# Paired GLA levels, mLSTM work on GpSimd, another projection weight and shifted pools in one encoder layer

## Chip, cores and metric

The kernel runs on one core of a Trainium2 chip. The metric is the device time of one launch in microseconds (us). Before the change it is 1205.28 us, the median of three runs (1203.65 to 1209.78).

## What is computed

One layer of an encoder over T = 1024 positions of width D = 1024 in float32. Token mixing and channel mixing follow each other, each with an RMS norm ahead and behind and a residual add:

```python
hn   = rms_norm(x, norm_mix_pre)
proj = hn @ w_in            # a_qk 512, a_v 512, a_o 512, a_gates 16, b_q 256, b_k 256, b_v 512, b_r 512, b_lr 32
# group A: 4 mLSTM heads (dk 64, dv 128), forward and backward, summed
qk  = silu(dwconv3(a_qk)); h_fw, h_bw = mlstm_chunkwise(...)
y_a = sigmoid(a_o) * head_rms_norm(h_fw + h_bw)
# group B: 4 GLA heads (dk 64, dv 128), forward and backward, summed
la  = log_sigmoid(lr @ w2 + gb) / 16
y_b = silu(b_r) * head_rms_norm(o_fw + o_bw)
x   = x + rms_norm(concat(y_a, y_b) @ w_out, norm_mix_post)
hn  = rms_norm(x, norm_ffn_pre)
x   = x + rms_norm((gelu(dwconv3(hn @ w_gate)) * (hn @ w_up)) @ w_down, norm_ffn_post)   # D_FF 2816
```

Within a chunk, GLA weighs each pair of positions (t, s) by exp(b_t - b_s) for each of the 64 key dimensions, where b is the running sum of the log gates:

```python
diff  = b[:, :, None, :] - b[:, None, :, :]
decay = exp(where(causal, diff, -inf))
s = einsum('td,sd,tsd->ts', q, k, decay)
o = s @ v + (q * exp(b)) @ S
```

mLSTM's weight of a pair is one number per head, exp(b_t - b_s + i_s - m_t), with a running maximum m and a normaliser n.

## The kernel before, in words

**Precision.** Most matmuls are done on splits: an operand becomes a high part in f32r and a low part with the rest (`split`, L109 to 111, a copy on ScalarE and a subtraction on VectorE), and a product is three matmuls, high by high, high by low, low by high.

**Stages.** The trace's span falls into these stretches: until 45 us the norm of x, its transposes into `xh`, `xl` and the first projection block (`wh0`, `wl0` from pool `s1`, L259); until about 455 us the rest of the projection, interleaved with the whole of the mixing; until 586 us the out projection (L975); until 991 us gate and up projection of the MLP; until the end at 1209 the down projection (L1194).

**The interleaved stage.** Two generators are run by `_interleave` (L42): `proj()` and `mix()`. Each holds a sum; the one with the lower sum gets the next step, and its weight is added. `proj()` has the weight 0.25. `mix()` starts with 1.0 and yields new weights on its way: `W_AUX` 0.85 for the decays and gates (`gla_decay`, `gate_rows`), `W_GLA` 0.19 for `gla()`, `W_ML` 0.26 for `mlstm()`, `W_OUT` 0.5 for `out_weights()`. A weight of 0.26 thus gives the projection 1.04 steps for each yield of the mix. `proj()` has 192 steps. Nearly each has matmuls: a `t_block` (L174) makes 48 matmuls of 128x256 for a pair of 128-row blocks in steps of 12, an `f_block` (L163) 24 of 128x512 in steps of 6. What the mix leaves over is run behind it, up to the point where the gate columns are done (`done["gate"]`), which the out projection's `prep(0)` needs.

The order in which steps are emitted gives priority; an instruction that is ready can be moved ahead of others on its queue, DMAs above all. Loads and stores through SP's queue (SPq in the profile) wait until the buffer that they fill is free.

**gate_rows** (L299) computes mLSTM's gate rows, stores two of them to DRAM (`drr`, `dri`) and, in its last step, transposes `gi`, `gf` and `rm` for eight chunks into `cols` (`ptc`, L369).

**gla()** (L543) has chunks of 128 positions: levels of chunk 0, then the states of all chunks, then for each chunk the levels of the next and its own `finish`. `levels(c)` cuts the 128x128 triangle into blocks: for L = 64, 32, 16, 8, 4, 2, 1 it pairs neighbouring blocks of L positions. A level has POOL subtract a reference column from the log sums X (`Dt`, L612), ScalarE take two exponentials of halves with opposite signs into the PSUM tile `E` (L616, L617), VectorE multiply E with q and k (`Q`; `K` or one of the zeroed `kz` tiles, L630). Then it yields, and TensorE makes the 32- or 64-wide score blocks `sc` (L649). These are merged into `acc` and `Pt` by copies and `copy_predicated`. The diagonal (k against q, without weights) follows level 1 in the same step. A chunk has eight yields. `finish(c)` makes `o`, copies it to `ob`, takes its head norm (ScalarE squares, a `pow` on POOL, L540, into `hr`) and stores it.

**mlstm()** (L696): `states()` makes chunk states (`Um`, L742). Then `front(c + 1)` and `back(c)` alternate, a yield behind each. `front` loads k, q and v and broadcasts rows into `RB` (128x1024, two directions) and `RI`; it makes the scores `sr` (L768), adds the causal mask `cap` (part of tile `cin`) to RB on VectorE (L769), takes eight exponentials on ScalarE (L772), multiplies by `sr` on VectorE (L773), and multiplies `RI` by q on VectorE (L775). `back` makes `nd` from RB and v and from RI and the states (L784, L788), divides into `hs` (ScalarE L799, VectorE L800), takes the head norm and stores to `dya`.

**out_weights()** (L828) loads w_out in eight pieces (`oraw`, L835) and splits them into `woh`, `wol` (L106, L107). Its pool `op` is opened when mlstm's pools are closed and lies over them. `prep(0)` (L846) then loads y (`yv`) and the gates (`gv` from `dG`), multiplies (L855), transposes (L861) and splits into `yh`, `yl`.

**The MLP** uses one level of a Strassen-like scheme. `strassen` (L1073) makes seven products of four by three matmuls 128x512 (`product`, L1036) for each of 22 operand sets. The moving operands are B11 and B21 (pool `bp`), T1 to T4 and B22 (pool `tp`); the stationary ones, `ah` and `al`, lie in pool `fw`.

**Where tiles lie.** Pools are opened on the left or (`side="right"`) on the right of each partition's memory. The left has `cst` (ident, one, hg, hr, mhalf), then `s1`, `mid`, `rw`, `gp`, the mix's `lp` pools, `op`, `pre`, `ering`, `tp`, `fk` and the down projection's pools, one over another as they close. The right has `xt`, `wp`, `rst`, `stg` and later `bp`, `fw`, `nt`. A tile that is made longer in `cst` moves all later pools on the left.

## Time and profile before

| | before |
|---|---|
| median of three runs | 1205.28 us |
| lowest, highest | 1203.65, 1209.78 us |
| profiled execution, run time | 1211.2 us |
| its span | 1209.4 us |
| mean granted clock of TensorE | 0.987 |
| TensorE busy, matmuls | 1166.3 us (96%), 7896 |
| VectorE busy | 895.2 us (74%) |
| ScalarE busy | 601.0 us (50%) |
| POOL busy | 129.6 us (11%) |
| DMA | 175.77 MB, mean 145 GB/s |

The profile is one execution. Busy time counts instructions that run; a wait stands with the instruction that came behind it and with what released it. TensorE's matmuls are pipelined, so the time of one is longer than the distance from one start to the next, and a rate is read from starts. The granted clock is a share of TensorE's full speed.

### The profile page before, as it was taken

The numbers are of one execution on the slowest core, as the hardware profiler recorded it, in microseconds if no ns is written. First come the engines' busy times: TensorE is split into PE (matmuls) and PEld (weight loads), VectorE is DVE, ScalarE is ACT, GpSimd is POOL, SyncE is SP. The second block draws the span as 40 slices with busy tenths as digits, with TensorE's granted clock in tenths as the row PEclk, the third lists the DMA queues.
The fourth block names the chain that finished last, engine by engine and source line by source line (L and its number), as shares of the span: only waits on it lengthen the run. The fifth ranks groups of instructions, "written<-read, shape, count | busy, mean of one in ns | idle before, by whom it ended". The sixth has DMA issues, their size and how long they took to land.

```text
span 1209.4 us, 21264 instructions
## 1 busy us (share of the span) xinstructions
PE 1166.3 (96%) x7896; PEld 985.8 (82%) x7896; DVE 895.2 (74%) x1620; ACT 601.0 (50%) x1327; POOL 129.6 (11%) x167
## 2 busy tenths in 40 slices
PE   8998999989988899999999999999999999999997
PEld 8988777878887898887788888888888878888885
DVE  5576689677365547667998887888878877987666
ACT  5573786778556534446543233323333335444451
POOL 1201433554001100111000000000000000000001
PEclk8998999999999999999999999999999999999999
DMA  7453675553677467442144332333224228854345
GB/s 193 151 140 89 191 212 143 149 153 107 192 207 191 147 215 245 140 157 79 35 140 139 105 114 63 129 114 114 72 94 131 96 81 306 266 166 140 87 135 187
DMA packets 134651, 175.77 MB, mean 145 GB/s; under 512 B 24964, under 2 KB 89860, under 8 KB 134548
## 3 DMA queue, kind: packets, MB, share of 16 engines
q1 hardware_dynamic: 134116, 172.58, 46.4%
q0 software_dynamic: 432, 1.84, 0.4%
q8 instruction: 62, 1.02, 0.3%
q14 instruction: 41, 0.34, 0.1%
HBM read 126.78 MB, written 47.53 MB: 144 GB/s over the span
## 4 chain that ended last, share of the span: by engine, by line
PE 69%; DMA 3%; DVE 3%; ACT 1%; issue 1%; SPq 0%; POOL 0%; DVEq 0%; POOLq 0%; ACTq 0%
PE pr L1036 35%; PE pr L1194 17%; PE tacc L180 7%; PE oacc L975 6%; DMA RB<-drr 1%; PE nd L784 1%; PE pt L861 1%; DMA yv<-dya 1%; ACT RB L772 1%; PE Um L742 1%; PE sc L649 0%; DMA qq<-dmqq 0%; PE sr L768 0%; DMA v<-dva 0%; DMA ar<-dA 0%
## 5 line engine op out<-in xcount | busy, mean ns | idle before, releaser
L1036 PE MATMUL pr<-T,ah 128*128 128x512 f32 x704 | 222.1, 397 | 1.1 <-DVE G L1074 1.1
L1036 PE MATMUL pr<-B,ah 128*128 128x512 f32 x528 | 164.3, 392 | 0.0
L1036 PEld LDWEIGHTS pr<-T,ah 128*128 128x128 f32 x704 | 132.4, 188 | 33.4 <-DVE G L1074 1.5
L1036 PE MATMUL pr<-T,al 128*128 128x512 f32 x352 | 139.5, 396 | 0.0
L180 PE MATMUL tacc<-wh,xh 128*128 128x256 f32 x448 | 133.1, 297 | 0.0
L180 PE MATMUL tacc<-wl,xh 128*128 128x256 f32 x448 | 131.0, 292 | 0.0
L180 PE MATMUL tacc<-wh,xl 128*128 128x256 f32 x448 | 130.5, 291 | 0.0
L1194 PE MATMUL pr<-dwl,dah 128*128 128x512 f32 x308 | 120.0, 390 | 0.7 <-DVE dwl L111 0.7
L1194 PE MATMUL pr<-dwh,dal 128*128 128x512 f32 x308 | 120.0, 389 | 0.0
L1194 PE MATMUL pr<-dwh,dah 128*128 128x512 f32 x308 | 119.1, 389 | 0.6 <-ACT dah L110 0.6
L1036 PEld LDWEIGHTS pr<-B,ah 128*128 128x128 f32 x528 | 99.1, 188 | 22.3
L1036 PE MATMUL pr<-B,al 128*128 128x512 f32 x264 | 103.4, 392 | 0.0
L110 ACT CAST dah<-ar 128x512 fp32r<-128x512 f32 x77 | 47.7, 622 | 98.3 <-PE pr L1194 46.9
L180 PEld LDWEIGHTS tacc<-wh,xh 128*128 128x128 f32 x448 | 88.1, 197 | 3.0 <-issue 0.2
L180 PEld LDWEIGHTS tacc<-wl,xh 128*128 128x128 f32 x448 | 88.3, 197 | 0.8
L180 PEld LDWEIGHTS tacc<-wh,xl 128*128 128x128 f32 x448 | 88.2, 197 | 0.6
L110 ACT CAST ah<-fraw 128x512 fp32r<-128x512 f32 x64 | 39.7, 620 | 86.4 <-PE pr L1036 58.0
L111 DVE TENSOR_TENSOR dal<-ar,dah 128x512 fp32r<-128x512 f32 x77 | 52.7, 687 | 38.5 <-ACT dah L110 38.5
L1036 PEld LDWEIGHTS pr<-T,al 128*128 128x128 f32 x352 | 66.3, 188 | 16.1
L110 ACT CAST ah<-sa 128x512 fp32r<-128x512 f32 x44 | 27.3, 621 | 87.1 <-PE pr L1036 51.2
L1194 PEld LDWEIGHTS pr<-dwh,dah 128*128 128x128 f32 x308 | 57.8, 188 | 13.0 <-ACT dah L110 1.0
L1194 PEld LDWEIGHTS pr<-dwl,dah 128*128 128x128 f32 x308 | 57.8, 188 | 12.9 <-DVE dwl L111 1.1
(294 smaller groups left out, 2520.5 us busy)
## 6 DMA issues: line engine op xcount, KB each, us to landing
ar<-dA SPq DMA_DIRECT2D x77, 256.0 KB
wraw<-in_w_in_dram SPq DMA_DIRECT2D x48, 256.0 KB
fraw<-in_ffn_w_gate_dram SPq DMA_DIRECT2D x22, 512.0 KB
fraw<-in_ffn_w_up_dram SPq DMA_DIRECT2D x22, 512.0 KB
dA<-s SPq DMA_DIRECT2D x20, 512.0 KB
dA<-sx SPq DMA_DIRECT2D x10, 768.0 KB
Y<-in_ffn_w_down_dram SPq DMA_DIRECT2D x22, 256.0 KB
S<-dS SPq DMA_DIRECT2D x16, 258.0 KB
```

The lines of the kernel that those rows point to most:

```text
L110: nc.scalar.copy(out=hi, in_=src)
L111: nc.vector.tensor_tensor(out=lo, in0=src, in1=hi.bitcast(F32), op=ALU.subtract)
L180: nc.tensor.matmul(acc[:, i, :], v[:, k, ts], w[:, k, :], start=(k == 0 and n == 0), stop=(k == NK - 1 and n == 2))
L742: nc.tensor.matmul(U[:, j, 0:P + 1], KT[:, 2 * g + j, :], v[:, 2 * g + j, :], start=True, stop=True)
L772: nc.scalar.activation(RB[:, i, h, :], RB[:, i, h, :], AF.Exp, bias=cols[:, c, 0, 32 * i + h:32 * i + h + 1])
L784: nc.tensor.matmul(nds[h // 2][i][:, h % 2, 0:P + 1], Ps[i][:, h, :], v[:, h, :], start=(h % 2 == 0), stop=False)
L861: nc.tensor.transpose(pt[:, j, :], yv[:, (4 * g + j) * P:(4 * g + j + 1) * P], ident)
L975: nc.tensor.matmul(accs[hf], v[:, j, :], w[:, k, hf * 512:(hf + 1) * 512], start=(k == 0 and n == 0), stop=(k == NK - 1 and n == 2))
L1036: nc.tensor.matmul(acc, A[i][:, k, :], B[b][j][:, k, :], start=(k == 0 and n == 0), stop=(k == 3 and n == 2))
L1194: nc.tensor.matmul(accs[i], o[v][:, ts], o[w], start=(p == 0 and n == 0), stop=(p == NP - 1 and n == 2))
```

## The change

There are five edits.

1. `levels(c)`: a level's subtraction is written as two of half the size with opposite signs, so that one exponential over the whole tile serves both halves. The score products of two levels are issued together, one step behind the weighing of the second (`products(due[:2])`), and their merges behind both. The diagonal counts as a level of its own with a yield of its own, so a chunk has nine yields. Q has three buffers, ob one.
2. `gate_rows` has one more yield ahead of the transposes.
3. `W_ML` is 0.36, which gives 1.44 projection steps a yield.
4. In mLSTM's `front`, the mask add on RB and the product of RI and q are on POOL.
5. A tile of 152 float32 (608 bytes a partition) is added to `cst`, one of 168 (672 bytes) to `s1`. Nothing uses them.

```diff
--- before.py
+++ after.py
@@ -34,7 +34,7 @@
 TEMP = 16.0
 BIG = 1e30
 
-W_AUX, W_GLA, W_ML, W_OUT = 0.85, 0.19, 0.26, 0.5
+W_AUX, W_GLA, W_ML, W_OUT = 0.85, 0.19, 0.36, 0.5
 C_AQK, C_AV, C_AO, C_AG = 0, 512, 1024, 1536
 C_BQ, C_BK, C_BV, C_BR, C_LR = 1552, 1808, 2064, 2576, 3088
 
@@ -100,6 +100,7 @@
     hg = cst.tile([P, NK, 1], F32, name="hg")
     hr = cst.tile([P, NC, 2, H], F32, name="hr")
     mhalf = cst.tile([P, 8], F32, name="mhalf")
+    cst.tile([P, 152], F32, name="shift")
     nc.gpsimd.memset(mhalf, -0.5)
 
     def split_scaled(hi, lo, src, g):
@@ -205,6 +206,7 @@
     sml = rst.tile([P, NT, 112], F32, name="sml")
     s1c = ExitStack()
     s1 = s1c.enter_context(tc.tile_pool(name="s1", bufs=2))
+    s1.tile([P, 168], F32, name="shift0", bufs=1)
     wh0 = s1.tile([P, NK, NS], F32R, name="wh0", bufs=1)
     wl0 = s1.tile([P, NK, NS], F32R, name="wl0", bufs=1)
     gpre = s1.tile([P, D], F32, name="gpre", bufs=1)
@@ -363,6 +365,7 @@
             nc.sync.dma_start(ddec[i], dcr[rs, :])
             nc.sync.dma_start(dec[64 * i:64 * i + 64], ddec[i].rearrange("(o h) c -> o h c", o=1).broadcast_to([64, H, NC]))
         yield
+        yield
         for c in range(NC):
             pt = ps.tile([P, 3, 36], F32, name="ptc", tag="ps")
             for j, z in enumerate((gi, gf, rm)):
@@ -572,7 +575,7 @@
                     v = v_tile(lp, dvb, c)
                     nc.scalar.activation(gam[:, c, :], S[:, :, P], AF.Exp, scale=1.0 / TEMP)
                     E = edge_decay(S, hi, lo)
-                    kd = w2k("Q")
+                    kd = w2k("Q", 3)
                     nc.vector.tensor_tensor(out=kd, in0=E, in1=kk, op=ALU.mult)
                     yield
                     pt = ps.tile([P, H, P], F32, name="ptk", tag="ps")
@@ -604,64 +607,79 @@
                 X = S[:, :, 0:P]
                 Pt = w2k("Pt")
                 acc = lp.tile([P, H, 32], F32, name="acc")
-                mi = 0
-                for L in (64, 32, 16, 8, 4, 2, 1):
-                    nb = P // (2 * L)
+                half = lambda z, i, L: z.rearrange("p h (n i j) -> p (h n) i j", i=2, j=L)[:, :, i, :]
+
+                def weigh(L):
+                    if L == 0:
+                        return qq, kk
                     Dt = w2k("D")
-                    xv = X.rearrange("p h (n j) -> p h n j", j=2 * L)
-                    nc.gpsimd.tensor_tensor(out=Dt.rearrange("p h (n j) -> p h n j", j=2 * L), in0=xv,
-                                            in1=xv[:, :, :, L:L + 1].broadcast_to([P, H, nb, 2 * L]), op=ALU.subtract)
+                    xv, dv = (z.rearrange("p h (n i j) -> p h n i j", i=2, j=L) for z in (X, Dt))
+                    ref = xv[:, :, :, 1, 0:1].broadcast_to([P, H, P // (2 * L), L])
+                    nc.gpsimd.tensor_tensor(out=dv[:, :, :, 0, :], in0=ref, in1=xv[:, :, :, 0, :], op=ALU.subtract)
+                    nc.gpsimd.tensor_tensor(out=dv[:, :, :, 1, :], in0=xv[:, :, :, 1, :], in1=ref, op=ALU.subtract)
                     E = pe.tile([P, H, P], F32, name="E", tag="pe")
-                    half = lambda z, i: z.rearrange("p h (n i j) -> p (h n) i j", i=2, j=L)[:, :, i, :]
-                    nc.scalar.activation(half(E, 0), half(Dt, 0), AF.Exp, scale=-1.0 / TEMP)
-                    nc.scalar.activation(half(E, 1), half(Dt, 1), AF.Exp, scale=1.0 / TEMP)
-                    Q = w2k("Q")
+                    nc.scalar.activation(E, Dt, AF.Exp, scale=1.0 / TEMP)
+                    Q, K = w2k("Q", 3), None
                     if L == 64:
                         nc.vector.tensor_tensor(out=Q, in0=E, in1=z64, op=ALU.mult)
-                    elif L == 32:
-                        nc.vector.tensor_tensor(out=Q, in0=E, in1=qq, op=ALU.mult)
+                        return Q, K
+                    nc.vector.tensor_tensor(out=Q, in0=E, in1=qq, op=ALU.mult)
+                    if L == 32:
                         K = w2k("K", 1)
                         nc.vector.tensor_tensor(out=K, in0=E, in1=kk, op=ALU.mult)
                     else:
-                        nc.vector.tensor_tensor(out=Q, in0=E, in1=qq, op=ALU.mult)
                         K = kz[L]
                         for i in range(2):
                             rs = slice(64 * i, 64 * i + 64)
-                            nc.vector.tensor_tensor(out=half(K[rs], i), in0=half(E[rs], i), in1=half(kk[rs], i), op=ALU.mult)
-                    yield
-                    if L == 64:
-                        sc = ps.tile([P, H, 64], F32, name="sc", tag="ps")
-                        for h in range(H):
+                            nc.vector.tensor_tensor(out=half(K[rs], i, L), in0=half(E[rs], i, L), in1=half(kk[rs], i, L), op=ALU.mult)
+                    return Q, K
+
+                def pair_up(L, Q, K):
+                    sc = ps.tile([P, H, 64 if L == 64 else 32], F32, name="sc", tag="ps")
+                    for h in range(H):
+                        if L == 64:
                             nc.tensor.matmul(sc[0:64, h, :], Q[0:64, h, 0:64], Q[0:64, h, 64:128], start=True, stop=True)
                             nc.tensor.matmul(sc[64:128, h, :], Q[64:128, h, 64:128], Q[64:128, h, 0:64], start=True, stop=True)
+                            continue
+                        for b in range(4):
+                            bs = slice(32 * b, 32 * b + 32)
+                            if L == 32:
+                                ob = slice(32 * (b ^ 1), 32 * (b ^ 1) + 32)
+                                rs = lo if b % 2 == 0 else hi
+                                nc.tensor.matmul(sc[bs, h, :], K[rs, h, bs], Q[rs, h, ob], start=True, stop=True)
+                            elif L == 0:
+                                nc.tensor.matmul(sc[bs, h, :], kk[:, h, bs], qq[:, h, bs], start=True, stop=True)
+                            else:
+                                nc.tensor.matmul(sc[bs, h, :], K[:, h, bs], Q[:, h, bs], start=True, stop=True)
+                    return sc
+
+                def keep(L, sc):
+                    if L == 64:
                         nc.scalar.copy(out=Pt[0:64, :, 64:128], in_=sc[0:64])
                         nc.scalar.copy(out=Pt[64:128, :, 0:64], in_=sc[64:128])
+                    elif L == 32:
+                        for b in range(4):
+                            ob = slice(32 * (b ^ 1), 32 * (b ^ 1) + 32)
+                            nc.scalar.copy(out=Pt[32 * b:32 * b + 32, :, ob], in_=sc[32 * b:32 * b + 32])
+                    elif L == 16:
+                        nc.scalar.copy(out=acc, in_=sc)
                     else:
-                        sc = ps.tile([P, H, 32], F32, name="sc", tag="ps")
-                        for h in range(H):
-                            for b in range(4):
-                                bs = slice(32 * b, 32 * b + 32)
-                                if L == 32:
-                                    ob = slice(32 * (b ^ 1), 32 * (b ^ 1) + 32)
-                                    rs = lo if b % 2 == 0 else hi
-                                    nc.tensor.matmul(sc[bs, h, :], K[rs, h, bs], Q[rs, h, ob], start=True, stop=True)
-                                else:
-                                    nc.tensor.matmul(sc[bs, h, :], K[:, h, bs], Q[:, h, bs], start=True, stop=True)
-                        if L == 32:
-                            for b in range(4):
-                                ob = slice(32 * (b ^ 1), 32 * (b ^ 1) + 32)
-                                nc.scalar.copy(out=Pt[32 * b:32 * b + 32, :, ob], in_=sc[32 * b:32 * b + 32])
-                        elif L == 16:
-                            nc.scalar.copy(out=acc, in_=sc)
-                        else:
-                            nc.vector.copy_predicated(acc, bmask[:, mi:mi + 1, :].broadcast_to([P, H, 32]), sc)
-                            mi += 1
-                sc = ps.tile([P, H, 32], F32, name="sc", tag="ps")
-                for h in range(H):
-                    for b in range(4):
-                        bs = slice(32 * b, 32 * b + 32)
-                        nc.tensor.matmul(sc[bs, h, :], kk[:, h, bs], qq[:, h, bs], start=True, stop=True)
-                nc.vector.copy_predicated(acc, bmask[:, mi:mi + 1, :].broadcast_to([P, H, 32]), sc)
+                        mi = (8, 4, 2, 1, 0).index(L)
+                        nc.vector.copy_predicated(acc, bmask[:, mi:mi + 1, :].broadcast_to([P, H, 32]), sc)
+
+                def products(pair):
+                    scs = [(L, pair_up(L, *qk)) for L, qk in pair]
+                    for L, sc in scs:
+                        keep(L, sc)
+
+                due = []
+                for n, L in enumerate((64, 32, 16, 8, 4, 2, 1, 0)):
+                    due.append((L, weigh(L)))
+                    if n % 2 == 0 and n:
+                        products(due[:2])
+                        due = due[2:]
+                    yield
+                products(due)
                 for b in range(4):
                     bs = slice(32 * b, 32 * b + 32)
                     nc.scalar.copy(out=Pt[bs, :, bs], in_=acc[bs])
@@ -678,7 +696,7 @@
                 for h in range(H):
                     nc.tensor.matmul(o[:, h, :], Pt[:, h, :], v[:, h, 0:P], start=True, stop=False)
                     nc.tensor.matmul(o[:, h, :], qd[:, h, :], slots[:, c, h, :], start=False, stop=True)
-                ob = w2k("ob")
+                ob = w2k("ob", 1)
                 nc.scalar.copy(out=ob, in_=o)
                 head_norm(lp, ob, dyb[c], 1, c)
                 yield
@@ -766,13 +784,13 @@
                 sr = ps.tile([P, H, P], F32, name="sr", tag="ps")
                 for h in range(H):
                     nc.tensor.matmul(sr[:, h, :], kk[:, h, :], qq[0:64, h, :], start=True, stop=True)
-                nc.vector.tensor_tensor(out=RB, in0=RB, in1=cap.rearrange("p (i o t) -> p i o t", i=2, o=1).broadcast_to([P, 2, H, P]), op=ALU.add)
+                nc.gpsimd.tensor_tensor(out=RB, in0=RB, in1=cap.rearrange("p (i o t) -> p i o t", i=2, o=1).broadcast_to([P, 2, H, P]), op=ALU.add)
                 for i in range(2):
                     for h in range(H):
                         nc.scalar.activation(RB[:, i, h, :], RB[:, i, h, :], AF.Exp, bias=cols[:, c, 0, 32 * i + h:32 * i + h + 1])
                 nc.vector.scalar_tensor_tensor(out=RB, in0=sr.rearrange("p (o h) t -> p o h t", o=1).broadcast_to([P, 2, H, P]), scalar=0.125, in1=RB, op0=ALU.mult, op1=ALU.mult)
                 Ps = [RB[:, i] for i in range(2)]
-                nc.vector.tensor_tensor(out=RI, in0=RI, in1=qq, op=ALU.mult)
+                nc.gpsimd.tensor_tensor(out=RI, in0=RI, in1=qq, op=ALU.mult)
                 live[c] = (Ps, RI, v)
 
             def back(c):
```

## Prediction

> **What bounds the kernel now.** I read the page's first line, then the busy time by stage (TensorE is PE), the waits of TensorE, the chain of waits, and single tiles on the timeline.
>
> ```profile
> span 1209.4 us, 21264 instructions
> ```
>
> The profiled run took 1211.2 us, 1.8 of them outside the span. The median of the three timed runs is 1205.28 us, so the profile lies 5.9 us above it: I work out differences on the profile and take them off the median. A measurement of this kernel can tell about 0.5%, 6 us, from no change.
>
> Busy time by stage (window, length, busy us of each engine, granted clock, DMA):
>
> ```profile
> core 0: us, PE busy (x) PEld busy (x) DVE busy (x) ACT busy (x) POOL busy (x), PEclk, DMA share, GB/s
> 104.80:120.00 15.20, 11.27 (x65) 10.60 (x65) 5.79 (x9) 6.93 (x16) 3.43 (x7) 0.66 0.34 97
> 120.00:180.00 60.00, 58.81 (x563) 46.91 (x562) 43.59 (x95) 46.68 (x100) 23.61 (x21) 1.00 0.71 201
> 180.00:304.00 124.00, 115.17 (x2322) 103.85 (x2321) 96.53 (x216) 93.80 (x272) 59.96 (x57) 1.00 0.48 141
> 304.00:345.00 41.00, 39.62 (x322) 37.20 (x321) 20.00 (x51) 24.13 (x67) 2.11 (x4) 1.00 0.70 197
> 345.00:413.40 68.40, 57.43 (x466) 52.88 (x465) 39.24 (x136) 39.72 (x148) 7.72 (x7) 0.93 0.64 175
> 413.40:455.00 41.60, 39.25 (x319) 38.48 (x318) 18.18 (x33) 16.09 (x27) 1.46 (x2) 0.98 0.60 197
> ...
> 586.00:991.00 405.00, 404.61 (x1741) 327.68 (x1742) 338.59 (x483) 150.57 (x216) 0.47 (x1) 1.00 0.31 102
> ```
>
> These are the gates, GLA (two rows), the mLSTM states, the mLSTM fronts and backs, the projection left behind mLSTM, and the gated MLP. In the MLP, TensorE is busy for 404.61 of 405 us: only cheaper matmuls count there. From 104.8 to 413.4 it idles 3.9 + 1.2 + 8.8 + 1.4 + 11.0 = 26.3 us, and the clocks 0.66 and 0.93 cost 0.34 × 15.2 + 0.07 × 68.4 = 10.0 us more. These 36.3 us are all that the mix can win. The waits between 100 and 460 us name them (total, times, longest):
>
> ```profile
> PE sc L649 <- DVE kz L630: 6.6, 7, 1.3
> PE sr L768 <- ACT hs L799: 5.4, 3, 3.3
> PE ptc L369 <- DVE gf L357: 3.9, 1, 3.9
> PE sr L768 <- DVE RB L773: 3.1, 1, 3.1
> PE nd L784 <- DVE hs L800: 2.5, 1, 2.5
> ```
>
> **More projection beside the mix.** From the yields and weights in the code: at mLSTM's last step 165 of the 192 projection steps have been handed out, after the change 187 (nine more yields at the GLA weight or before it, then 1.44 instead of 1.04 projection steps a yield). Behind mLSTM stand 27 steps before, 26 with matmuls, and 5 after, 4 with matmuls. The difference is 22 matmul steps; I take 21 as pulled in front, one for the error of such counting. The chain of waits prices a step and shows the rest:
>
> ```profile
> 345.22 1.80 PE nd L784 x16
> ...
> 348.81 6.11 DMA RB<-drr
> ...
> 355.01 1.24 DVE RB L769
> ...
> 356.27 2.46 ACT RB L772 x8
> ...
> 413.44 37.27 PE tacc L180 x309
> ...
> 455.31 6.19 PE oacc L975 x24
> ```
>
> 37.27 / 309 = 0.1206 us a matmul, 12 a step: 21 steps are 30.4 us of work ahead of mLSTM's end, which stands at 413.4. Without idle time and clock loss it would be at 413.4 − 36.3 + 30.4 = 407.5. What stays of the 36.3:
>
> *Gates, 9.1.* The wait of 3.9 us for gf is followed by the low clock of that row. The extra yield puts 0.85 / 0.25 = 3.4 projection steps, 4.9 us, ahead of the transposes: it covers the wait. I keep 2 for what is next late.
>
> *GLA, 10.0.* A level's subtraction becomes two of half the size, its two exponentials one, and its product is issued a yield or two later.
>
> ```profile
> L612 POOL TENSOR_TENSOR D<-S x56: 1040/1050/2584, 120.3 to 294.3; 128x512 f32<-128x512 f32 x56
> ```
>
> The two halves cost POOL 1.05 us (elements alone) to 2.1 (start alone). At 56 levels the upper end adds 59 us to 83.6 busy in 184, which still fits. I take 1.3, nearer to the elements, since one exponential less pays for the rest. One yield more gives 0.76 × 1.45 = 1.1 us against waits of at most 1.3: I keep 3 (0 to 10: a third Q and two score tiles in the same three PSUM buffers could also cost what the yield wins). The single ob costs nothing: its norm and store of one chunk are over long before the next chunk's nine yields are; without that cover it would wait for a store, some 4 us a chunk as yv's transfer below.
>
> *mLSTM states, 1.4.* I keep 0.5.
>
> *Fronts and backs, 11.0 idle and 4.8 clock.* nd of one chunk ends at 345.22 + 1.80 = 347.02 and frees the RB that the front two chunks on loads. The score product of the front after that needs the PSUM buffer which that RB's multiplication frees:
>
> ```profile
> 356.64 0.28 PE L180 MATMUL tacc<-wh,xl 128*128 128x256 f32 x1
> ...
> 360.03 1.16 PE L768 MATMUL sr<-qq,kk 64*128 64x128 f32 x8 [3.11 <-DVE RB L773]
> ...
> 361.93 0.41 PE L180 MATMUL tacc<-wh,xh 128*128 128x256 f32 x1
> ```
>
> The chain is 360.03 − 347.02 = 13.0 us, 9.9 covered and 3.11 idle; after it the matmul of 0.28 takes 0.41, the clock is lowered. The change gives three yields' 0.4 steps more, 3 × 0.4 × 1.45 = 1.7, so 11.6 covered; the mask add goes to POOL:
>
> ```profile
> L769 DVE TENSOR_TENSOR RB<-RB,cin x8: 1215/1225/1226, 335.0 to 402.1; 128x1024 f32<-128x1024 f32 x8
> ```
>
> On POOL it is 2 × 1.05 = 2.1 by the subtraction of half its size, 0.9 more: chain 13.9, idle 2.3, or 0.74 of before. The Trainium skill (GPSIMD Engine Reference, 3.1 Elementwise — side-by-side cycle accounting) keeps elementwise work on VectorE and gives 1.96 times VectorE's time, which speaks against the move: by an estimate from that, 2.4 us, 0.3 more a chain and about 1 us in the sum. VectorE loses the eight adds and these eight products,
>
> ```profile
> L775 DVE TENSOR_TENSOR RI<-RI,qq x8: 681/684/692, 340.3 to 403.8; 128x512 f32<-128x512 f32 x8
> ```
>
> 8 × (1.225 + 0.684) = 15 of its 39.24 us, so its own wait, 2.5 on hs L800, goes. The waits on ScalarE's hs and on RB keep 0.74 × (5.4 + 3.1) = 6.3; the clock keeps half, 2.5. On POOL's queue, behind an add that waits for its DMA, stand the same chunk's RI product (1.05 there, done while ScalarE takes 2.46; without that cover 0.4 a chunk, 3 in all) and the pow of the chunk before, read only in the out projection: nobody waits for either. POOL goes from 7.7 to some 33 of 68 us.
>
> Kept: 2 + 3 + 0.5 + 6.3 + 2.5 = 14.3; mLSTM ends at 421.8 (410 to 430).
>
> **The start of the out projection.** With 4 matmul steps left, what decides is the chain behind mLSTM's end:
>
> ```profile
> L835 SPq DMA_DIRECT2D oraw<-in_w_out_dram x8: 327/328/1700, 418.0 to 436.3; - x8
> ```
> ```profile
> L848 SPq DMA_DIRECT2D yv<-dya x3: 319/327/1232, 440.6 to 457.2; - x3
> L855 DVE SCALAR_TENSOR_TENSOR yv<-gv,hr,yv x15: 344/346/351, 452.6 to 459.9; 128x128 f32<-128x128 f32 x15
> ```
> ```profile
> 518.26 4.13 DMA yv<-dya
> ```
>
> w_out's space overlays mLSTM's tiles, so its loads start 4.6 us behind 413.4 and yv's read follows at 440.6, 27.2 behind. With 0.8 for two issues (0.33 and one a little longer), 4.13 to land and 2.7 to gate, transpose and split (452.6 to 455.31), the first product could start 34.8 behind; in the trace that was hidden by the 37.27 us of projection. With no projection loads and stores beside it, it may shrink to 28; I take 31.5, about the middle. TensorE then runs dry for 31.5 − 5.8 = 25.7 us and restarts at the low clock, for which I add 2. Start: 421.8 + 33.5 = 455.3, against 455.31. So the mix, which sheds 22 us of its waits, wins nothing: the idle time moves behind mLSTM.
>
> **The shift.** From the tile sizes, all pools on the left start 608 bytes later, 9.5 × 64. T1 to T4 and B22 are on the left and lie 32 bytes off a multiple of 64; ah and al, B11 and B21 are on the right at multiples of 64. The MLP's products in order of time:
>
> ```profile
> 745.40 0.63 PE L1036 MATMUL pr<-T,ah 128*128 128x512 f32 x2
> ...
> 753.84 0.63 PE L1036 MATMUL pr<-B,ah 128*128 128x512 f32 x2
> ...
> 756.64 0.63 PE L1036 MATMUL pr<-B,ah 128*128 128x512 f32 x2
> ...
> 759.39 0.62 PE L1036 MATMUL pr<-B,ah 128*128 128x512 f32 x2
> ...
> 762.11 0.63 PE L1036 MATMUL pr<-T,ah 128*128 128x512 f32 x2
> ```
>
> 36 matmuls with T take 8.44 us, 234.4 ns each; 12 with B22 2.80, 233; 12 with B11 2.75, 229; 12 with B21 2.72, 227. What T and B22 share is the other phase of 64 bytes; B22 is split from a load like B11, so fresh sums of VectorE are not it. The shift brings all five to ah's phase: 22 sets × 5 products × 12 = 1320 matmuls × 7.5 ns = 9.9 us, all on the bound engine. The first projection block also pairs a left wh0 with a right xh, in phase today:
>
> ```profile
> 29.76 0.30 PE L259 MATMUL vacc<-wh,xh 128*128 128x304 f32 x1
> 31.01 0.30 PE L259 MATMUL vacc<-wh,xh 128*128 128x304 f32 x1
> ```
>
> Nine intervals in 1.25 us, 139 ns for 304 columns, lie on the line between 121 at 256 and 227 at 512: no excess. The 672 bytes in s1 make its shift 20 × 64, which keeps it so. Out and down products have both operands on the left; the transposes against the unmoved identity change phase, at most 64 × 7.5 ns = 0.5 us in the out projection. From below, the saving is nothing, if phase isn't the cause.
>
> Sum: 0 − 9.9, 1205.3 − 9.9 = 1195.
>
> **Rivals.**
>
> *The shift doesn't pay, the change doing nothing there (0.2).* Then the excess comes from VectorE's work or from the ends of a set, and the time is 1205. For it: only one kernel's placement is in the trace, and B11 is 2 ns above B21 in the same pool. Against: the step between B22 and B11 with nothing else changed. [...]
>
> *The mix's waits vanish (0.2).* mLSTM ends at 410, out starts at 443.5, 11.8 earlier: 1205.3 − 21.7 = 1184. For it: VectorE and ScalarE sit at 57% of the mLSTM row, so covers may do all. Against: the 13 us chain of DMA, POOL and ScalarE.
>
> *TensorE runs dry at the out projection (0.1, slower).* Projection that filled the time of w_out's loads is spent, and the mix keeps its waits because they aren't a matter of cover: with all 36.3 kept mLSTM ends at 443.8 and out starts at 477.3, +22.0 − 9.9 = +12: 1217. It is slower by over 6 us when mLSTM ends later than 437.7. Against: 0.4 steps a yield are real cover.
>
> **How the numbers follow.** The forecast has 0.5: 1195, by itself 1184 (mLSTM's end at 410) to 1204 (at 430); a tenth of that lies within 0.5%. Faster: 0.45 + 0.2 = 0.65; same: 0.05 + 0.2 = 0.25; slower: 0.10. The range 1181 to 1208 takes in the forecast, the vanished waits and the shift that doesn't pay, and leaves out the dry start and the tails.
>
> **What would show it.** T's and B22's matmuls 227 to 229 ns apart and the MLP stage 10 us shorter (else the shift rival); some 60 tacc matmuls and no more behind mLSTM's end; that end near 422; TensorE idle some 25 us ahead of oacc at about 455; the gf wait gone; RB's add about 2.1 us on POOL. An end of mLSTM before 412 or behind 437 makes the forecast wrong, as does an oacc that starts under 28 us behind it.

## The result and the profile after

The changed kernel takes 1218.05 us, the median of five runs (1214.52 to 1221.87); the kernel before 1204.03 us in five runs on the same chip. The ratio is 1.0109, 95% interval 1.0074 to 1.0144: slower, by 13 us. The forecast was 1195, the range ended at 1208. The profiled execution took 1220.6 us. That is 2.6 above its median, while the profiled execution of the kernel before (1211.2) lies 7.2 above the median of the five, so the two profiles are only 9.4 us apart.

```profile
span 1218.9 us, 21251 instructions
```

Two things happened, and they pull apart. From the first to the last product of the MLP and the down projection the kernel before takes 644.2 us, the changed one 634.0: 10 us won. But the first product of the out projection starts at 473.5 instead of 455.0, 18.5 later. With 1.0 us more between the out projection's first product and the MLP's first (104.0 against 103.0), 18.5 + 1.0 - 10.2 = 9.3 is the difference of the two spans (9.5) but for 0.2. The rows of the busy time by stage show both. The stages have moved, so the rows are cut anew: gates, GLA (two), states, fronts and backs, the wait for the out projection, and the MLP in a stretch 10 us shorter than the one shown before.

```profile
104.80:120.00 15.20, 10.18 (x73) 9.44 (x72) 4.62 (x7) 5.99 (x14) 2.76 (x6) 0.78 0.42 116
120.00:176.50 56.50, 54.58 (x524) 43.62 (x524) 40.20 (x85) 43.38 (x86) 18.25 (x25) 1.00 0.70 204
176.50:306.00 129.50, 121.43 (x2369) 110.18 (x2367) 102.82 (x226) 87.25 (x226) 75.29 (x111) 0.97 0.48 137
306.00:355.00 49.00, 49.00 (x410) 47.41 (x410) 11.86 (x31) 28.46 (x77) 9.41 (x8) 1.00 0.64 182
355.00:443.70 88.70, 75.79 (x603) 70.87 (x601) 37.22 (x142) 38.91 (x144) 28.62 (x19) 0.90 0.52 144
443.70:473.50 29.80, 9.28 (x68) 8.39 (x68) 16.08 (x31) 13.38 (x23) 1.01 (x1) 0.68 0.79 249
...
606.00:1001.00 395.00, 395.00 (x1743) 327.05 (x1744) 337.14 (x483) 149.89 (x215) 0.73 (x1) 1.00 0.32 105
```

From 104.8 to mLSTM's end, now at 443.7, TensorE idles 5.0 + 1.9 + 8.1 + 0 + 12.9 = 27.9 us. It was 26.3. Its busy time in these rows is 311.0 us; it was 282.3. So mLSTM's end is 30.3 us later by 28.7 of work and 1.6 of idle time. The granted clock fell in the fronts and backs (0.93 before, 0.90 now) and in the second GLA row (1.00, 0.97) and rose in the gates (0.66, 0.78), but the sum leaves nothing over for it. The waits that the change was to cover have not gone; they have other names, as the waits of TensorE between 100 and 500 us show (its largest groups):

```profile
PE pt L879 <- DVE yv L873: 20.5, 1, 20.5
PE sr L786 <- DVE RB L791: 12.5, 5, 5.0
PE ptc L372 <- ACT cols L373: 5.0, 1, 5.0
PE sc L651 <- issue: 3.4, 2, 2.3
PE sc L641 <- DVE Q L624: 3.3, 1, 3.3
PE sc L653 <- DVE kz L634: 1.3, 2, 0.7
```

And the first line is new: 20.5 us in which TensorE has nothing at all. The chain of waits tells what it waits for:

```profile
443.70 7.39 PE tacc L181 x60
...
454.16 3.56 DMA oraw<-in_w_out_dram
...
457.74 1.16 ACT woh L107
...
458.92 1.30 DVE wol L108
...
460.23 4.29 DMA oraw<-in_w_out_dram
...
464.55 1.16 ACT woh L107
...
465.73 1.30 DVE wol L108
...
467.04 4.02 DMA yv<-dya
...
471.14 1.67 DVE yv L873 x6
...
473.68 0.60 PE oacc L993
```

Of the 309 projection matmuls behind mLSTM, 60 are left. They end at 451, and w_out's loads, which could only start when mLSTM's tiles were free, run until yv can be read at 467. They don't run in one stream: the eight pieces of `oraw`, yv and gv share three buffers, so a load waits until the piece before it in its buffer has been split on ScalarE and VectorE (`woh`, `wol`), and yv's read waits for such a split too. mLSTM's end is later by about what the 249 matmuls (30.0 us) pulled ahead of it take. No wait that went paid for them.

### The profile page after: what moved, and what is told of

It reads as the page before. It is cut to its first block, busy times and chain, and to the rows that moved or that the text cites. A ratio compares the mean times of both kernels' runs of the same rounds, so it can differ in the third digit from the quotient of the medians.

```text
span 1218.9 us, 21251 instructions
## 1 busy us (share of the span) xinstructions
PE 1153.6 (95%) x7896; PEld 983.9 (81%) x7896; DVE 884.3 (73%) x1604; ACT 591.3 (49%) x1271; POOL 165.6 (14%) x239
## 4 chain that ended last, share of the span: by engine, by line
PE 58%; DVE 3%; DMA 2%; ACT 1%; issue 1%; POOL 0%; SPq 0%; DVEq 0%; POOLq 0%; ACTq 0%
PE pr L1054 34%; PE pr L1212 15%; PE oacc L993 6%; PE tacc L181 1%; DMA yv<-dya 1%; DMA oraw<-in_w_out_dram 1%; PE pt L879 1%; DVE x L1245 0%; DMA RI<-dri 0%; PE nd L802 0%; PE pt L971 0%; DVE xr L1014 0%; DVE wol L108 0%; DMA ar<-dA 0%; DVE yv L873 0%
## 5 line engine op out<-in xcount | busy, mean ns | idle before, releaser
L1054 PE MATMUL pr<-T,ah 128*128 128x512 f32 x704 | 217.0, 389 | 1.3 <-DVE G L1092 1.3
L1054 PE MATMUL pr<-T,al 128*128 128x512 f32 x352 | 137.0, 389 | 0.0
L1212 PEld LDWEIGHTS pr<-dwh,dal 128*128 128x128 f32 x308 | 57.8, 188 | 12.7 <-DVE dal L112 0.7
```

The source lines that it names most:

```text
L1054: nc.tensor.matmul(acc, A[i][:, k, :], B[b][j][:, k, :], start=(k == 0 and n == 0), stop=(k == 3 and n == 2))
L1212: nc.tensor.matmul(accs[i], o[v][:, ts], o[w], start=(p == 0 and n == 0), stop=(p == NP - 1 and n == 2))
```

## The experiments

All ratios are to the kernel before on the same chip, with 95% intervals. "Stretch" is the fronts and backs from the first to the last `nd` matmul, "end" the start of that last one, "out" the first `oacc`, "idle" TensorE's idle time between the two, "MLP" first to last product of the last two stages, all in us from each run's one profile. In kernels whose instructions stand in the same order before the out projection the stretch varies by several us between executions (63.7 to 70.0 in three runs that only move tiles, with the kernel before at 68.1), so a difference of 3 us there says little.

```
run              ratio   interval          stretch  end    out    idle  MLP
before           1                          68.1    413.2  455.0   2.4  644.2
after            1.0109  1.0074 to 1.0144   78.2    443.4  473.5  20.5  634.0
e1_after_w26     0.9960  0.9942 to 0.9979   73.1    428.8  461.5   4.5  634.1
e2_after_noshift 1.0185  1.0160 to 1.0210   79.3    445.1  476.5  21.8  643.7
e3_shift_only    0.9906  0.9880 to 0.9932   64.9    409.6  450.5   1.5  633.7
e4_before_w36    1.0035  1.0019 to 1.0051   67.5    422.4  454.6   9.7  644.5
e5_after_vec     1.0026  1.0010 to 1.0042   69.6    434.8  464.6  20.2  633.9
e6_paired_bal    0.9884  0.9859 to 0.9909   66.1    406.7  446.4   0.5  634.4
e7_shift640      0.9984  0.9966 to 1.0001   70.0    413.9  452.8   0    642.9
e8_shift608_s1in 0.9902  0.9872 to 0.9932   63.7    406.3  446.9   1.1  634.5
e9_after_ripool  1.0073  1.0049 to 1.0097   71.6    436.9  466.7  20.2  633.7
e10_paired_nogate 0.9913 0.9886 to 0.9940   67.6    406.4  448.5   0.3  633.9
e11_paired_split 0.9906  0.9889 to 0.9924   71.2    407.1  447.6   0.3  633.9
e12_after_qq3    1.0087  1.0069 to 1.0105   78.9    443.3  472.4  19.6  634.9
e13_after_qq8    1.0022  1.0008 to 1.0036   66.8    429.8  458.6  19.3  634.6
e14_bal_qq8      0.9922  0.9898 to 0.9945   64.3    406.2  447.0   1.0  634.1
```

**The tail: weights.** These two runs change mLSTM's weight alone: does the time follow the projection that is left behind mLSTM?

```diff
 after.py
-W_AUX, W_GLA, W_ML, W_OUT = 0.85, 0.19, 0.36, 0.5
+W_AUX, W_GLA, W_ML, W_OUT = 0.85, 0.19, 0.26, 0.5
```

> The changed kernel with mLSTM's weight back at 0.26, all else kept. Tail theory (the out projection starts 30 us behind mLSTM's last step, as after the change, and projection pulled ahead of that step is missing behind it): 19 steps stay behind instead of 5, 14 x 1.45 = 20 us leave mLSTM's stretch, its last nd starts near 425 instead of 443.4, TensorE idles a few us instead of 20.5 ahead of the out projection, which starts near 455; time 1196 to 1201. Cover theory (the slowdown comes from the mask add and the RI product on POOL and from the paired levels, and the higher weight is what limits it): mLSTM's waits grow by 10 us and more, time 1216 to 1228.

0.9960 is 1199 on the scale of 1204. The end moved to 428.8 and TensorE idled 4.5 us ahead of the out projection. 216 matmuls, 18 steps, stood there. Putting one number back takes 18 us off the changed kernel.

```diff
 before.py
-W_AUX, W_GLA, W_ML, W_OUT = 0.85, 0.19, 0.26, 0.5
+W_AUX, W_GLA, W_ML, W_OUT = 0.85, 0.19, 0.36, 0.5
```

> The kernel before with mLSTM's weight at 0.36 alone. Tail theory: 13 steps instead of 27 stay behind mLSTM, its last nd starts at 413 + 20 less up to 6 of its waits, 428 to 433, the out projection 30 us later at 458 to 463, TensorE idle some 10 us ahead of it: 1207 to 1212. Cover theory: the waits of the fronts and backs fall by half or more and nothing is lost behind: 1197 to 1201.

1.0035, 1208: the tail theory's time. It was right in the 9.7 us of idle, too late in the end, 422.4 instead of 428 to 433, and in the start of the out projection, 454.6 instead of 458 to 463. So its time came in partly by luck: in the profile the out projection starts no later than before, and 1.4 us are lost between its first product and the MLP's (104.4 against 103.0). More projection per yield does cover waits in the fronts and backs of this kernel: their idle fell from 11.0 to 6.3 us. Both theories had a part, but what was covered there came back behind.

Over the four kernels the out projection starts 30.1 (60 matmuls left), 32.2 (168), 32.7 (216) and 41.8 us (309) behind mLSTM's end. Below some 200 matmuls it doesn't follow the work that is left, but the loads and the splits between them.

**The placement.** These four runs take the unused tiles away or add them alone.

```diff
 after.py
-    cst.tile([P, 152], F32, name="shift")
-    s1.tile([P, 168], F32, name="shift0", bufs=1)
```

> The changed kernel without the two unused tiles. If the operands' placement is what made the MLP stage 10 us shorter (644.2 to 634.0 us from its first to its last product): 1228, matmuls with T and B22 234 ns apart again. If the stage got shorter for another reason (the different timing of what stands ahead of it): 1218.

The same two lines, added to the kernel before:

> The kernel before with the two unused tiles alone. Placement theory: all stages up to the out projection as before, T and B22 matmuls 227 to 229 ns apart, 10 us saved: 1194. Rival: 1204, 234 ns.

```diff
 before.py
+    cst.tile([P, 160], F32, name="shift")
```

> The kernel before with one unused tile of 640 bytes (10 x 64) in the pool cst, none in s1. Phase theory: a move by a multiple of 64 bytes changes nothing, T and B22 matmuls stay 234 ns apart, MLP stage 644 us, 1204. Rival (the distance moved or the place in memory counts, not the phase): 227 ns and 1194.

```diff
 before.py
+    cst.tile([P, 152], F32, name="shift")
```

> The kernel before with the tile of 608 bytes alone, none in s1: s1's weights now lie on the other phase from xh. Phase theory: T and B22 at 227 ns, MLP stage 634; the first block's 192 matmuls of 304 columns, now across phases, start 143 to 147 ns apart instead of 140, 1 us lost: 1195. If only the operand of 512 columns suffers: 140 ns, 1194.

Without the tiles the MLP takes 643.7 again and the time is 1.0185, 1226 on the scale of 1204 (1228 was expected); with nothing but them the MLP takes 633.7, and 640 bytes instead of 608 leave it at 642.9. So it is not a move as such that counts, but the 32 bytes by which 608 is off a multiple of 64. Only this one offset was tried. The profile pages' groups of the products with T (mean ns of one matmul), first without the tiles, then with both, then with 640 bytes:

```profile
L1052 PE MATMUL pr<-T,ah 128*128 128x512 f32 x704 | 222.1, 397 | 1.1 <-DVE G L1090 1.1
```
```profile
L1038 PE MATMUL pr<-T,ah 128*128 128x512 f32 x704 | 217.1, 389 | 1.3 <-DVE G L1076 1.3
```
```profile
L1037 PE MATMUL pr<-T,ah 128*128 128x512 f32 x704 | 221.3, 395 | 1.1 <-DVE G L1075 1.1
```

On the timeline of the changed kernel, 36 matmuls lie between these two, 8.16 us, 226.7 ns each; it was 234.4:

```profile
760.20 0.39 PE L1054 MATMUL pr<-T,al 128*128 128x512 f32 x1
...
768.36 0.39 PE L1054 MATMUL pr<-T,al 128*128 128x512 f32 x1
```

With 608 bytes and no tile in s1, the first block's matmuls of 304 columns lie across the phases and still start 140 ns apart (139 before). The rival of that run is right: only the matmul of 512 columns pays for it here, and the second tile does nothing that can be measured (0.9902 against 0.9906).

**mLSTM's operations on POOL.** These four runs put one or both operations back on VectorE, or give q more buffers.

```diff
 after.py, front(c)
-                nc.gpsimd.tensor_tensor(out=RB, ...)
+                nc.vector.tensor_tensor(out=RB, ...)
...
-                nc.gpsimd.tensor_tensor(out=RI, ...)
+                nc.vector.tensor_tensor(out=RI, ...)
```

> The changed kernel with the mask add and the RI product back on VectorE, weight 0.36 and the rest kept. Chain theory: the fronts and backs are set by a loop over two chunks (nd frees RB, loads of 1.7 + 6.1 us, add, eight exponentials, multiplication, nd), which POOL's add of 2.36 us instead of 1.22 lengthens: that stretch shrinks from 78 to 67-69 us, as with 0.36 alone on the kernel before (67.5), TensorE's idle in it from 12.9 to 5-7; mLSTM ends at 433, the out projection starts at 463; time 1206 to 1209 where the kernel before is at 1204. Filler theory (the stretch got longer by the projection put into it): 76-78 us, 1216.

1.0026: the stretch shrinks from 78.2 to 69.6, the out projection starts 8.9 us earlier. The chain theory gave the numbers, but for a reason that did not last, as the next runs show. VectorE was not slowed by POOL's work beside it: its multiplication of RB takes 1.225 us at the median of the fronts and backs of the kernel before and of the changed one alike.

The first of the two edits alone:

> The changed kernel with the mask add back on VectorE and the RI product left on POOL. Chain theory: only the add lies in the loop that sets the fronts and backs; the RI product runs beside the exponentials. That stretch is 69 to 71 us, as with both on VectorE (69.6), out projection at 464 to 466; 1.002 to 1.004 of the kernel before. If RI on POOL is what hurts (it takes 1.27 us and is read by the second half of nd): 74 to 78 us and 1.007 to 1.011.

1.0073, the rival's time, but not the rival's stretch: 71.6 is near the 69 to 71 of the chain theory and within what executions differ by. By the ratio the RI product on POOL keeps about half of the loss, although it is no part of the chain from RB's load to `sr`. The profiles don't bear that out: the out projection starts only 2.1 us later than with both on VectorE, and q's load waits 7.0 us for that product, 6.2 with both on VectorE. The two runs were on different chips; what the product costs alone stays open. But by its ratio the chain theory lacks something, and for the changed kernel itself SP's queue has it. Its waits in the fronts and backs of the changed kernel (355 to 444 us):

```profile
SPq L544 <- DVE hs L818: 23.0, 7, 8.0
SPq L520 <- POOL RI L793: 18.7, 4, 5.2
SPq L776 <- PE sr L786: 7.8, 4, 4.0
```

and of the kernel before (345 to 414), where line 517 is that load of q:

```profile
SPq L517 <- DVE RI L775: 4.1, 1, 4.1
```

q has two buffers, and the next load of q needs the one that the RI product reads. On POOL this product stands behind the add, and the timelines of POOL and of SP in the changed kernel show what follows:

```profile
409.34 2.36 POOL L787 TENSOR_TENSOR RB<-RB,cin 128x1024 f32<-128x1024 f32 x1 [1.10 <-DMA qq<-dmqq]
411.65 1.27 POOL L793 TENSOR_TENSOR RI<-RI,qq 128x512 f32<-128x512 f32 x1
422.42 2.37 POOL L787 TENSOR_TENSOR RB<-RB,cin 128x1024 f32<-128x1024 f32 x1 [9.50 <-DMA RB<-drr]
```
```profile
412.95 1.08 SPq L520 DMA_DIRECT2D qq<-dmqq  x2
414.12 1.18 SPq L514 DMA_DIRECT2D v<-dva  x1
415.39 1.05 SPq L782 DMA_DIRECT2D RB<-drr  x2
```

The product ends at 412.92, q's load goes out at 412.95, and v's and RB's loads go behind it on the same queue. The add of the next chunk then waits 9.50 us for RB.

```diff
 after.py, front(c)
-                qq = load(lp, "qq", dmqq[c])
+                qq = load(lp, "qq", dmqq[c], 3)
```

> The changed kernel with a third buffer for mLSTM's q tile, all else kept, both operations on POOL. Queue theory: the RI product on POOL runs behind the add (2.36 us) and in two chunks of eight behind a pow; q's next load waits for it at the head of SP's queue, and the loads of v and RB stand behind that load, so that they start 3 to 4 us later than nd allows. With a third buffer they start when nd ends: the fronts and backs take 72 to 75 us instead of 78, the out projection starts at 468 to 470, 1.004 to 1.007 of the kernel before. Rival (only the longer add in the chain counts): stretch 77 to 79, 1.009 to 1.012.

Nothing: 1.0087, stretch 78.9. But this run did not take the wait away. A third buffer let the load of q be issued a chunk earlier, and it waited for the latest RI product all the same, at the head of the queue (15.4 us in three waits). It tells nothing of the queue theory.

```diff
 after.py, front(c)
-                qq = load(lp, "qq", dmqq[c])
+                qq = load(lp, "qq", dmqq[c], 8)
```

> The changed kernel with eight buffers for mLSTM's q tile, so that no load of q waits for the RI product any more (with three, the load was only issued a chunk earlier and stood in front of the queue all the same). Queue theory: RB's loads start when nd ends, not up to 4 us later; the fronts and backs take 71 to 75 us instead of 78, their idle 7 to 10 instead of 12.9; the out projection starts at 466 to 470; 1.003 to 1.007 of the kernel before. Rival (POOL's longer add alone makes the stretch longer, the queue's wait is hidden): 77 to 79 us, 1.009 to 1.012.

With a buffer for each chunk all loads of q are issued by 357 us, and the waits for the RI product are gone from SP's queue. What SP waits for in front of RB's loads (364 to 440 us) is now nd, which v's load needs:

```profile
SPq L514 <- PE nd L802: 11.8, 4, 4.0
```

The stretch is 66.8, the idle in it 6.3 instead of 12.9, the out projection starts at 458.6, 14.9 earlier (11.4 of it are the stretch), and the ratio is 1.0022: more than expected. The add is still on POOL:

```profile
L787 POOL TENSOR_TENSOR RB<-RB,cin x8: 2350/2364/2393, 329.1 to 418.4; 128x1024 f32<-128x1024 f32 x8
```

So the queue's wait was the loss. The longer add by itself can't be seen: in four cases of five the time from nd's end to the score product three chunks on is 12.8 to 13.1 us, no more than before. No run has both operations on VectorE beside eight buffers and the weight 0.36, so the add's own price isn't measured. The 19.3 us of idle ahead of the out projection stay: the tail is a matter of its own.

**What is left: paired levels, the gates' yield, where the projection stands.** Each of these is the changed kernel with both operations on VectorE and the weights such that 26 to 28 steps stay behind mLSTM.

```diff
 after.py, with both operations on VectorE
-W_AUX, W_GLA, W_ML, W_OUT = 0.85, 0.19, 0.36, 0.5
+W_AUX, W_GLA, W_ML, W_OUT = 0.85, 0.17, 0.26, 0.5
```

> The changed kernel with both operations on VectorE, mLSTM's weight 0.26 and GLA's 0.17, so that again 27 steps stay behind mLSTM: what is left of the change is the paired levels, the gates' yield and the shift. If the paired levels are worth nothing: the same as the shift alone, 0.9906 of the kernel before, GLA's time besides projection at 75 us as in all runs so far. If pairing does save waits and they were spent elsewhere: 3 to 7 us less, 0.985 to 0.988, GLA at 68-72.

0.9884, between the two forecasts, and its interval holds the 0.9906 of the tiles alone. GLA's time besides projection (from its first score product to its last `o`, less the spacing of the projection's matmuls, 0.1206 us for each tacc and 0.2275 for each facc) is 73.0 us, against 75.6 and 74.3 in the two runs with tiles alone. Over all profiles it is 72.0 to 75.3 in the eleven with paired levels and 74.3 to 75.6 in the five without, on average 1 us less. So the pairing is worth about 1 us, if anything, and the runs can't tell that from nothing in the time.

```diff
 e6, gate_rows
         yield
-        yield
         for c in range(NC):
```

> The balanced version (both operations on VectorE, weights 0.17 and 0.26, shift) without the extra yield of the gates. Theory: the yield exchanges a wait for gf of 3.9 us for one of 5 us, behind a weight cast on ScalarE that waits for its load; without it the wait for gf is back, 3.5 to 4, the one of 5 gone, about 1 us and nothing to be measured: 0.987 to 0.990. Rival (the yield is worth what it was to bring): 3 to 4 us slower, 0.991 to 0.993.

0.9913: in the rival's range, but the interval reaches into the other as well, so the time doesn't decide. The profile shows the wait for gf back at 3.7 us and the one of 5 us gone, as expected.

```diff
 e6, mLSTM's weights
-        yield W_ML
+        yield 0.18
         yield from mlstm()
...
             front(0)
-            yield
+            yield 0.36
```

> The balanced version with the weight 0.18 in the mLSTM states and 0.36 in its fronts and backs, so that the projection stands where the waits are and as much as before stays behind. Tail and chain theories together: fronts and backs 67 to 70 us long with 17 to 18 steps in them instead of 13, their idle 4 to 6 us instead of 8.7, states shorter by as much projection, mLSTM's end 2 to 4 us earlier with 26 or so steps behind it: 0.985 to 0.987. If the waits only move into the states: 0.988 to 0.990.

0.9906: nothing gained, a miss. 16.7 steps stood in the fronts and backs, but they idled 8.4 us, as e6's 8.7. More projection there covered nothing this time, unlike in e4; why not isn't settled.

```diff
 e6, front(c)
-                qq = load(lp, "qq", dmqq[c])
+                qq = load(lp, "qq", dmqq[c], 8)
```

> The balanced version (both operations on VectorE, weights 0.17 and 0.26, paired levels, shift) with eight buffers for q. If q's load holds up RB's there too (4.1 us of such waits in the kernel before): fronts and backs 62 to 65 us instead of 66, 0.984 to 0.988. If not: 0.988 to 0.991.

0.9922: with the RI product on VectorE q's load is no limit, and the eight buffers bring nothing. The six fastest versions (e3, e6, e8, e10, e11, e14) have the shift and 26 to 28 steps behind mLSTM in common, and can't be told apart: 0.988 to 0.992. Two of them are the kernel before with a tile or two added, so of the five edits only the shift is shown to gain.

## Why the prediction was wrong, step by step

**The shift** was right: 9.9 us forecast, 10.2 measured between the two profiles; the last two stages take 642.9 to 644.5 us in the four profiles out of phase and 633.7 to 634.9 in all others. The cause was tested (e2, e3, e7). The rival that the shift doesn't pay has fallen. The second tile, for which the prediction saw a reason in the first block, had none (e8).

**The tail's price** was near: 31.5 + 2 us forecast from mLSTM's end to the out projection, 30 measured; 21 steps pulled ahead forecast, 20.75 measured (249 matmuls); 25.7 us of idle forecast, 20.5 measured. The 2 for the restart at a low clock can't be seen: from the out projection's first product to the MLP's first it is 1.0 us more, and the runs spread over 102.2 to 106.6 there.

**What stays of the 36.3 us** is the step that failed. "Kept: 2 + 3 + 0.5 + 6.3 + 2.5 = 14.3; mLSTM ends at 421.8". It ended at 443.7; with all kept, the prediction had 443.8. Where 26.3 us were idle before, 27.9 were afterwards. The prediction's way of pricing the clock isn't borne out: by it the rows would lose 16.1 us to the clock after the change instead of 10.0, yet the busy time rose by 28.7 us, no more than the added matmuls take. Term by term:

- Gates: "it covers the wait. I keep 2". The wait for gf went, and 5.0 us came in its place. ScalarE's timeline has it:

```profile
113.84 0.62 ACT L111 CAST wh<-wraw 128x512 fp32r<-128x512 f32 x1 [5.35 <-DMA wraw<-in_w_in_dram]
114.36 0.54 ACT L373 COPY cols<-ptc 128x108 f32<-128x108 f32 x3
```

The extra projection put a weight cast in front of the copies of `ptc`. ScalarE waits 5.35 us for the weight's load, the copies stand behind it, and the transposes have three PSUM buffers. The prediction looked at what the yield puts on TensorE and not at what it puts on ScalarE's queue.

- GLA: "I keep 3 (0 to 10)". 10.0 were kept. The waits for kz fell from 6.6 to 1.3 us, and 3.3 us before one chunk's first Q and 3.4 before the diagonal's scores came. The two subtractions took 0.64 and 0.62 us at the median, 1.26 for 1.3 forecast. The prediction's own upper end held; the value within it did not.

- Fronts and backs: "nobody waits for either". That is the sentence that was wrong, on the RI product. q's load waits for it at the head of SP's queue, and RB's load behind that; e13, where this wait is gone, has a stretch 11.4 us shorter. The prediction kept 6.3 us of idle time here; 12.9 were measured. The chain was priced as 13.9 us with 0.9 more for the add. From nd's end to the score product three chunks on, the last four take 16.8 to 17.7 us; before, all but one took 12.9 to 13.5, and the one that the 4.1 us of q's wait hit took 16.5. The clock, 0.93 before, fell to 0.90 instead of gaining. The last of the four begins with nd's end at 412.30 and ends with this product:

```profile
429.23 2.07 PE L786 MATMUL sr<-qq,kk 64*128 64x128 f32 x8 [4.96 <-DVE RB L791]
```

The Trainium skill's ratio for POOL (GPSIMD Engine Reference, 3.1 Elementwise — side-by-side cycle accounting) was nearer than the row that I took: the estimate from it was 2.4 us for the add, and the trace has 2.364 against 1.225 on VectorE, 1.93 times; the prediction had 2.1. But this price was not what mattered.

**The rival "TensorE runs dry at the out projection"** is what happened, at its far end: mLSTM's end at 443.7 (its worst case 443.8), the time 1218 (1217 there). It had 0.1. That the numbers agree so closely is partly luck: it has the old waits stay, and here several of them went (gf, most of kz) and new ones of the same sum came. Its argument against itself, "0.4 steps a yield are real cover", was true of the kernel before (e4: idle 11.0 to 6.3). With both operations on POOL it was not: the fronts and backs idle 13.4 us at the weight 0.26 (e1) and 12.9 at 0.36. The chance was too small: a forecast of zero for the mix was the difference of two large numbers, 30 us moved and 22 us of waits shed, and the second rested on four terms of which each had to come true.

## What to carry to other kernels

Work that is pulled ahead of a point, to fill waits there, is missing behind it: look first for what starts at that point and how long it takes, and leave that much work behind. When an operation moves to another engine, follow not only who reads its result but which buffer it frees, which load waits for that buffer, and what stands behind that load on its queue. Where a matmul of 512 columns repeats some ns too slow for one set of tiles only, compare the addresses of its operands modulo 64.

## What the runs showed of the hardware

- A matmul 128x512 in f32r whose moving operand lies, by the tile sizes, 32 bytes off the phase (modulo 64) of its stationary one starts 234 ns after the one ahead, 227 in phase: 3%. Shifts of 608 bytes remove it, of 640 do not. At 304 columns there is no such difference (139 and 140 ns).
- POOL takes 2.36 us to add 128x1024 and 1.27 to multiply 128x512, where VectorE takes 1.225 and 0.684; a subtraction of 128x512 with a broadcast operand takes POOL 1.05.
